# First stage in three pieces with a written TensorE order, and earlier loads in the second attention, in a two-layer decoder trunk

## Chip, cores and metric

The kernel runs on one core of a Trainium2 chip. The metric is the device time of one execution in microseconds (us), the median of several runs. Three runs of the kernel before took 2381.39, 2383.12 and 2384.1 us; the median is 2383.12 us.

## The reference

Input is x, 1024 tokens by 1024 features, in float32, with a conditioning vector c. Two layers follow each other: an mLSTM layer with a squared-ReLU MLP, then a causal latent attention (MLA) layer with another MLP. What the change touches is the first projection of layer 0, and the start of the attention for the second half of the queries.

```python
cond = jax.nn.silu(c)
ada = cond @ ada_w[l] + ada_b[l]
sh1, sc1, g1, sh2, sc2, g2 = jnp.split(ada, 6, axis=-1)
h = modulate(rmsnorm(x, norm_g[l, 0]), sh1, sc1)     # rmsnorm(x) * g * (1 + sc1) + sh1
proj = h @ w_in                                      # q, k, v, gates, output gate
...
s = q_nope . k_nope + q_rope . k_rope                # per head, causal, softmax, times v
```

So before the first product of `proj` stand: the mean square of each token's row of x, the vectors sc1 and sh1 (each a product of cond with a 1024 x 1024 block of `ada_w`, 4 MB), and x with features on the partitions (x transposed).

## The kernel before, in words

The tokens are worked in two halves of 512 (`hfs[0]`, `hfs[1]`). Activations lie with features on partitions: eight blocks of 128 features by 512 tokens. Each float32 factor is split in a high part (rounded to fp32r) and a low part (the rest), and a product is three matmuls, `mm3` (L234 to L236): activation high by weight low, activation low by weight high, high by high. `wsplit` (L190) makes the parts of a weight block of 128 x 1024: ScalarE casts it (L192), VectorE subtracts (L193). `split_mod` (L470) does the same for an activation: ScalarE scales and rounds (L476), VectorE makes the low part (L477).

The order of each engine's instructions is made by a scheduler from the order of the program, from priorities and from `tc.issue_after`, which keeps an instruction behind another of the same engine. All loads and stores of this text are issued by SyncE (SP) in one queue, in order; a DMA waits there for the landing of the one eight places ahead of it, and for the buffer that it writes. Buffers come from pools: `k4` (24 of 4 KB a partition), `hd` (8), `raw` (4, weights as loaded), `ws` (8, weight parts), `tmc`, `tmp`, `tma`, and in PSUM `ps` (2 banks), `pc` (2 banks), `pm` (2 of 2 banks).

Stage one, up to the last row of `qk_pairs` (L572):
- `load_x(0)` (L293) loads four blocks of 128 tokens by 1024 features, 512 KB each. `rms_x0` (L507) squares each on ScalarE; `along_tokens` (L490, L495) lays the token's factor along the free dimension.
- `first_norm` (L1680): 32 transposes on TensorE (`turn`, L530), four to a PSUM bank of `pc`; ScalarE copies each bank out (L1687).
- `ada_first(j)` (L1671) for j = 0 and 1, each for 512 of the 1024 features. The sum for sc1 (SC1) is made on VectorE, `ada_chunk` (L351): eight accumulating operations of 128 x 512 (L361, L363), after which four one-column matmuls with `ones` add over the partitions (`ada_turn`, L336). The sum for sh1 (SH1) is made on TensorE, `ada_chunk_pe` (L316, L324). The loads of both alternate.
- `modulate0(j)` (L1690): for each of four blocks of features a multiplication on VectorE (L1697), then `split_mod`.
- `qk_pairs` (L572): six accumulators of 128 x 512 (q0 to q3, k0, k1; four in `pm`, two in `ps`), first over the four feature blocks of j = 0, then over those of j = 1, from three pairs of weight blocks of 256 columns: 144 matmuls.

`vector_columns` (L280) transposes the rows of norm gains and biases (st1, st2) into columns. After stage one the transposed x is stored to memory (L1773), and gates, the last q and k, v and the chunks follow.

The second attention: `attention_second` (L1559) prepares the second half's k, v and queries of the eight heads in pairs (`prepare_pair`, L1415). A pair stores its parts of k (kd, L1430), of v (vd, L1436), of the queries (qd, L1452) and of the rotary queries (td, L1453). After the fourth pair, `units` takes the heads one by one; `loaded_head` (L1460) loads all of a head's k (two loads, L1465), its queries (L1467), for an even head the pair's rotary queries (L1470), and v (two loads, L1473). The first score products (L1368 to L1374) read these. Dense MLP products of the first half are put between the steps of the attention.

Of the kernel before, what the change touches and what calls it, by code (L numbers as in the profile page):

```python
# [82 lines left out]
def kernel(  # L83
# [51 lines left out]
    def tmp(dt=F32):  # L135
        return sb.tile([P, 512], dt, tag="tmp", bufs=TMP, name=f"tmp_{next(uid)}")
# [91 lines left out]
    def wcols(w, c0, n=P, k0=0, nk=KD):  # L228
        return w[k0 * P : (k0 + nk) * P, c0 : c0 + n].rearrange("(k p) n -> p k n", p=P)
# [47 lines left out]

    cols = const([P, 200], F32, "cols")

    def vector_columns():  # L280
        for i, st in ((0, st1), (1, st2)):
            pt = ps()
            nc.tensor.transpose(pt[:, :P], st[:, :P], ident)
            n = min(P, 200 - i * P)
            nc.vector.tensor_copy(cols[:, i * P : i * P + n], pt[:, :n])

    col = lambda i, n: cols[:, i : i + n]
    NG = lambda l, i: col(l * 32 + i * 8, 8)
# [24 lines left out]
    ada = const([P, 2, 48], F32, "ada")  # L313
    kvada = const([P, 16], F32, "kvada")

    def ada_chunk_pe(w, c0, bias, dst, buf):  # L316

        rows = pc()
        for q in range(4):
            r = buf()[:, :1024].rearrange("p (a b) -> p a b", b=512)  # L320
            nc.sync.dma_start(r, wcols(w, c0, 512, 2 * q, 2))
            for kk in range(2):
                k = 2 * q + kk
                nc.tensor.matmul(  # L324
                    rows[ts(k % 4, 32)], condw[:, k], r[:, kk], start=k < 4, stop=k >= 4
                )
            yield
        acc = tmp()
        nc.scalar.copy(acc, rows)
        yield from ada_turn(acc, bias, dst, True)  # L330

    def ada_turn(acc, bias, dst, alone):
        pt = pc()
        if alone:
            for j in range(4):
                ada_last[0] = nc.tensor.matmul(  # L336
                    pt[:, j : j + 1], acc[:, ts(j, P)], ones[:, 0:1], start=True, stop=True
                )
            ada_sum[0] = nc.vector.tensor_add(dst, pt[:, :4], bias)
            yield  # L340
            return
        for j in range(4):
            ada_last[0] = nc.tensor.transpose(pt[:, ts(j, P)], acc[:, ts(j, P)], ident)
# [5 lines left out]
    ada_last, ada_sum = [None], [None]  # L349

    def ada_chunk(w, c0, bias, dst, buf=raw):  # L351

        acc = tma() if buf is raw else tmc()
        for q in range(4):
            r = buf()[:, :1024].rearrange("p (a b) -> p a b", b=512)
            nc.sync.dma_start(r, wcols(w, c0, 512, 2 * q, 2))
            for kk in range(2):
                k = 2 * q + kk
                with paced():
                    if k == 0:  # L360
                        nc.vector.tensor_scalar(acc, r[:, kk], cond[:, 0:1], None, ALU.mult)  # L361
                    else:
                        nc.vector.scalar_tensor_tensor(  # L363
                            acc, r[:, kk], cond[:, k : k + 1], acc, ALU.mult, ALU.add
                        )
            yield
        if buf is raw:
            yield
            yield "wait"
        yield from ada_turn(acc, bias, dst, buf is not raw)  # L370

    def ada_part(l, part, buf=raw, js=(0, 1), how=ada_chunk):
        for j in (2 * part + js[0], 2 * part + js[-1])[: len(js)]:
            yield from how(
                ada_w[l], j * 512, col(AB + l * 48 + j * 4, 4), ada[:, l, ts(j, 4)], buf
            )

    def ada_kv(part):
# [111 lines left out]
    def along_tokens(dst, y):  # L490


        pt = pc()
        for t in range(4):
            nc.tensor.matmul(  # L495
                pt[:, ts(t, P)], y[:, t : t + 1].to_broadcast([P, P]), ident, start=True, stop=True
            )
        nc.scalar.copy(dst, pt)
        return dst
# [68 lines left out]

    def w_qk(b, kh, load=wload):
        return load([(0, 0, wcols(w_in, b * 256, 256, 4 * kh, 4))], 256)  # L570

    def qk_pairs(hf, w0, ahead):  # L572


        h = hf.h
        hf.q = [k4v(), k4v()]
        hf.k = [k4v(), k4v()]
        m0, m1 = pm(), pm()
        acc = [(m0[:, 0], m0[:, 1]), (m1[:, 0], m1[:, 1]), (ps(), ps())]

        def half(b, kh, w):
            for r in range(2):
                for k in range(4):
                    kk = 4 * kh + k
                    mm3(
                        acc[b][r], w[0][:, k, ts(r, P)], w[1][:, k, ts(r, P)], h.hi[kk], h.lo[kk],
                        kk == 0, kk == KD - 1,
                    )

        half(0, 0, w0[0])  # L590
        with tc.issue_after(ada_last[0].ins):
            for b in range(1, 3):
                half(b, 0, w0[b])
        yield from ahead
        for b in range(3):
            half(b, 1, w_qk(b, 1, wload_late))
            for r in range(2):
                qk_evac(hf, 2 * b + r, acc[b][r])
            yield

    def qk_last(hf):
        h, acc = hf.h, (ps(), ps())
# [1065 lines left out]

    A0 = mods[:, 0]

    def ada_first(j, buf):  # L1671

        a_, b_ = ada_part(0, SC1, buf, (j,)), ada_part(0, SH1, buf, (j,), ada_chunk_pe)
        yield from weave(a_, b_, 1.0)
        s = ts(j, 4)
        nc.vector.scalar_tensor_tensor(
            A0[:, s], adac(0, SC1)[:, s], 1.0, NG(0, 0)[:, s], ALU.add, ALU.mult
        )

    def first_norm():  # L1680

        y = rms_x0(x0)
        xT = FH(claim=True)
        for k in range(KD):
            pt = pc()
            turn(x0, pt, k)
            nc.scalar.copy(xT[k], pt)  # L1687
        return xT, along_tokens(Cst.rearrange("p a b -> p (a b)")[:, :H], y)

    def modulate0(h, xT, j):  # L1690
        A, sh = A0, adac(0, SH1)

        behind = [None, ada_sum[0].ins]
        for k in range(4 * j, 4 * j + 4):
            u = tmc()
            with tc.issue_after(behind[k % 4]) if behind[k % 4] else nullcontext():
                nc.vector.scalar_tensor_tensor(u, xT[k], A[:, k : k + 1], rs0, ALU.mult, ALU.mult)  # L1697
            split_mod(h.hi[k], h.lo[k], u, sh[:, k : k + 1])
            behind.append(nc.cur_bb.bb.instructions[-1])
            yield  # L1700

    def w_raw(b):
        r = raw()
        nc.sync.dma_start(
            r.rearrange("p (a b) -> p a b", b=256), wcols(w_in, b * 256, 256, 0, 4)
        )
        return r

    def w_parts(r):
        return [t.rearrange("p (a b) -> p a b", b=256) for t in wsplit(r, D)]  # L1710

    vector_columns()
    xT0, rs0 = first_norm()
    drain(ada_first(0, k4))

    w0 = [w_raw(b) for b in range(3)]
    hfs[0].h = Split()
    w0[0] = w_parts(w0[0])
    drain(modulate0(hfs[0].h, xT0, 0))
    traced = nc.cur_bb.bb.instructions  # L1720
    with tc.issue_after(next(i for i in reversed(traced) if i.engine == dve)):
        w0[1:] = [w_parts(r) for r in w0[1:]]
    drain(ada_first(1, hd))

    def with_bg(g, bg, n):
        acc = 0.0
# [41 lines left out]
        drain(wide)  # L1768

    bgs = chain(bg0, bg1)  # L1770
    drain(qk_pairs(hfs[0], w0, modulate0(hfs[0].h, xT0, 1)))
# [239 lines left out]
```

## Time and profile before

| what | value |
|---|---|
| runs, median | 2383.12 us |
| profiled execution, its own time | 2388.66 us |
| its span | 2386.9 us |
| mean granted clock of TensorE | 0.996 |
| idle before the first transposes (x), four times | 3.8 us |

The page gives the busy time of each engine: PE is TensorE's matmuls, PEld its weight loads, DVE VectorE, ACT ScalarE, POOL GpSimd, and SPq SyncE's queue of DMA issues. A row of a timeline has start and duration in us, engine, line, operation, output <- inputs, shape and count, and in brackets the idle time before it and what ended it. A row of busy time by stretch has the stretch, its length, then for each engine (PE, PEld, DVE, ACT, POOL) busy us and the number of instructions, then the granted clock, the DMA engines' busy share and GB/s. A matmul's duration covers its way through the array, so rows that follow each other overlap; the distance of their starts is the pitch.

### The profile page before, as it was taken

What the parts mean: (1) busy time and instruction counts of PE and PEld (TensorE: products, weight loads), DVE (VectorE), ACT (ScalarE), POOL (GpSimd) and SP (SyncE); (2) the same over time, 40 slices, a digit from 0 to 9 for tenths busy, and PEclk for the clock granted to TensorE, in tenths of its full rate; (3) what the DMA queues carried; (4) which work ended last, traced back from release to release, by engine and by line L of the source; (5) the groups of instructions that cost most, each with busy time, mean ns of one, the idle gap of its engine ahead of it and who ended that gap; (6) DMA issues with size and microseconds to landing.
All of it is one profiled execution on the core that took longest, in us unless ns stands there. A gap on an engine that the chain in (4) does not pass through costs nothing.

```text
span 2386.9 us, 30478 instructions
## 1 busy us (share of the span) xinstructions
PE 2356.2 (99%) x11585; PEld 1939.7 (81%) x11585; DVE 1542.5 (65%) x2430; ACT 1057.0 (44%) x1726; POOL 17.0 (1%) x91
## 2 busy tenths in 40 slices
PE   8999999999999999999999999999999999999998
PEld 5888888888878887888888788878888888888886
DVE  6666776868665768777765877656666495353345
ACT  4354435655333454443443554434444353444333
POOL 1000000000000000000000000000000000000000
PEclk9999999999999999999999999999999999999999
DMA  8543454545563845555543544764434354354431
GB/s 309 170 126 111 143 171 142 168 139 161 176 193 109 273 152 167 166 155 174 178 133 116 164 160 152 252 230 135 137 98 156 102 166 133 102 185 141 145 98 62
DMA packets 376563, 372.91 MB, mean 156 GB/s; under 512 B 24323, under 2 KB 282432, under 8 KB 376416
## 3 DMA queue, kind: packets, MB, share of 16 engines
q1 hardware_dynamic: 376128, 370.86, 49.6%
q8 instruction: 91, 1.49, 0.3%
q14 instruction: 56, 0.46, 0.1%
q0 software_dynamic: 288, 0.10, 0.0%
HBM read 312.19 MB, written 58.72 MB: 155 GB/s over the span
## 4 chain that ended last, share of the span: by engine, by line
PE 85%; DMA 6%; DVE 5%; ACT 2%; issue 2%; SPq 0%; DVEq 0%; ACTq 0%
PE ps L234 16%; PE ps L235 15%; PE ps L236 15%; PE pm L234 9%; PE pm L235 9%; PE pm L236 9%; DMA raw<-in_mlp_w_dram 4%; DVE wl L193 1%; PE pc L1488 1%; ACT wh L192 1%; DVE tma L363 1%; PE pm L1374 1%; PE pc L234 1%; PE pc L235 1%; PE pc L236 1%
## 5 line engine op out<-in xcount | busy, mean ns | idle before, releaser
L193 DVE TENSOR_TENSOR wl<-raw,wh 128x1024 fp32r<-128x1024 f32 (+3 forms) x368 | 439.2, 1197 | 446.5 <-ACT wh L192 444.0
L192 ACT CAST wh<-raw 128x1024 fp32r<-128x1024 f32 (+3 forms) x368 | 376.8, 1028 | 731.6 <-PE ps L234 374.2
L234 PE MATMUL ps<-k,wl 128*128 128x512 f32 x1496 | 597.8, 400 | 1.0 <-DVE wl L193 0.9
L236 PE MATMUL ps<-k,wh 128*128 128x512 f32 x1496 | 588.1, 393 | 0.0
L235 PE MATMUL ps<-k,wh 128*128 128x512 f32 x1496 | 587.2, 392 | 0.0
L234 PEld LDWEIGHTS ps<-k,wl 128*128 128x128 f32 x1496 | 281.0, 188 | 65.9 <-issue 2.7
L236 PEld LDWEIGHTS ps<-k,wh 128*128 128x128 f32 x1496 | 280.9, 188 | 65.9 <-issue 0.2
L235 PEld LDWEIGHTS ps<-k,wh 128*128 128x128 f32 x1496 | 281.4, 188 | 61.8 <-issue 1.4
L201 DVE TENSOR_TENSOR k<-k,pm 128x512 f32<-128x512 f32 (+1 forms) x254 | 211.1, 859 | 97.0 <-PE pm L236 96.4
L234 PE MATMUL pm<-hd,wl 128*128 128x512 f32 x512 | 201.5, 394 | 0.4 <-ACT hd L473 0.4
L236 PE MATMUL pm<-hd,wh 128*128 128x512 f32 x512 | 200.1, 391 | 0.0
L235 PE MATMUL pm<-hd,wh 128*128 128x512 f32 x512 | 199.8, 391 | 0.2 <-DVE hd L474 0.2
L234 PE MATMUL pm<-wh,hd 128*128 128x512 f32 x488 | 192.5, 394 | 1.7 <-ACT raw L1380 1.3
L235 PE MATMUL pm<-wl,hd 128*128 128x512 f32 x488 | 191.2, 392 | 0.0
L236 PE MATMUL pm<-wh,hd 128*128 128x512 f32 x488 | 190.2, 390 | 0.0
L363 DVE SCALAR_TENSOR_TENSOR tma<-raw,cond,tma 128x512 f32<-128x512 f32 x168 | 125.5, 747 | 25.5 <-DMA raw<-in_kv_ada_w_dram 13.3
L474 DVE TENSOR_TENSOR hd<-tmp,hd 128x512 fp32r<-128x512 f32 x128 | 88.3, 690 | 53.7 <-ACT hd L473 53.3
L1380 ACT ACTIVATE raw<-pm,sm 128x128 f32<-128x128 f32 (+3 forms) x64 | 47.5, 742 | 155.0 <-DVE sm L1379 121.0
L234 PEld LDWEIGHTS pm<-hd,wl 128*128 128x128 f32 x512 | 96.1, 188 | 21.9 <-ACT hd L473 0.8
L235 PEld LDWEIGHTS pm<-hd,wh 128*128 128x128 f32 x512 | 96.1, 188 | 21.5 <-DVE hd L474 0.5
L236 PEld LDWEIGHTS pm<-hd,wh 128*128 128x128 f32 x512 | 96.1, 188 | 20.7
L234 PEld LDWEIGHTS pm<-wh,hd 128*128 128x128 f32 x488 | 91.6, 188 | 23.0 <-ACT raw L1380 3.8
(350 smaller groups left out, 3451.7 us busy)
## 6 DMA issues: line engine op xcount, KB each, us to landing
raw<-in_mlp_w_dram SPq DMA_DIRECT2D x256, 512.0 KB, 4.2
raw<-in_ada_w_dram SPq DMA_DIRECT2D x80, 512.0 KB, 4.3
raw<-in_a_w_in_dram SPq DMA_DIRECT2D x44, 512.0 KB, 4.3
xs<-k SPq DMA_DIRECT2D x40, 256.0 KB, 4.5
raw<-in_a_w_out_dram SPq DMA_DIRECT2D x16, 512.0 KB, 4.8
raw<-in_kv_ada_w_dram SPq DMA_DIRECT2D x16, 512.0 KB, 3.9
kd<-k SPq DMA_DIRECT2D x32, 256.0 KB, 4.3
vd<-k SPq DMA_DIRECT2D x32, 256.0 KB, 4.7
```

Of the source, the lines that this page charges most:

```text
L192: nc.scalar.copy(hi[:, :n], r[:, :n])
L193: i = nc.vector.tensor_sub(lo[:, :n], r[:, :n], hi[:, :n].bitcast(F32))
L201: return f(*a, **k)
L234: nc.tensor.matmul(o, ll, rh, start=start, stop=False)
L235: nc.tensor.matmul(o, lh, rl, start=False, stop=False)
L236: pe_last[0] = nc.tensor.matmul(o, lh, rh, start=False, stop=stop)
L363: nc.vector.scalar_tensor_tensor(acc, r[:, kk], cond[:, k : k + 1], acc, ALU.mult, ALU.add)
L474: nc.vector.tensor_sub(lo, u, hi.bitcast(F32))
L1374: nc.tensor.matmul(o[:, :w], qh, kh, start=False, stop=True)
L1380: nc.scalar.activation(pr[:, :n], f, AF.Exp, bias=m, scale=SCALE, accum_out=l)
L1488: nc.tensor.transpose(pt[:, ts(2 * e + i, P)], u.prs[i][:, ts(b + e, P)], ident)
```

## The change

1. x of the first half is loaded in eight half blocks (first all four blocks' features 0 to 511, then 512 to 1023). The banks of the 32 transposes come from `pc` and `ps` in turn, and VectorE, no longer ScalarE, copies them out.
2. `busy(14)`: 14 bf16 matmuls of `identb` with itself, 128 x 512, whose result nothing reads, at the start of TensorE's program.
3. Stage one goes by pieces of 256, 256 and 512 features (p0, p1, p2) instead of two of 512. For each piece the loads of SC1 and SH1 alternate; the first two pieces' blocks are 256 columns wide. p0's two sums are both made on TensorE; of p1 and p2, SC1's on VectorE and SH1's on TensorE. The six accumulators are filled piece by piece: the four q tiles from weight blocks of 512 columns by two feature blocks (wA), the two k tiles from blocks of 256 columns by four (wB). TensorE's order is written out with `on_pe`. All eight blocks of SC1 and SH1 loads of p2, then the four stores of the transposed x, stand ahead of the last three weight blocks in SP's queue.
4. st2 is transposed in the middle of the stage, in a bank of `pc`; `along_tokens` takes a bank of `ps` (for the second half, too).
5. In `attention_second` the loads of head 0 are traced after the fourth pair's kd stores and ahead of its vd, qd and td stores.

The program's order on the engines after stage one is otherwise that of before.

```diff
     def load_x(half):
-        xt = []
-        for t in range(4):
-            a = k4()[:, :1024]
-            nc.sync.dma_start(a, x_of[half * 4 + t])
-            xt.append(a)
+        xt = [k4()[:, :1024] for _ in range(4)]
+        for g in range(2):
+            for t in range(4):
+                nc.sync.dma_start(xt[t][:, ts(g, 512)], x_of[half * 4 + t][:, ts(g, 512)])
         return xt
...
     def along_tokens(dst, y):
-        pt = pc()
+        pt = ps()
...
             else:
-                yield from pairs[p_]
+                yield next(pairs[p_])
+                first = loaded_head(0)
+                yield from pairs[p_]
 
         def units():
             for hh in range(NH):
-                h_ = loaded_head(hh)
+                h_ = loaded_head(hh) if hh else first
...
+    def first_turn():
+        xT = FH(claim=True)
+        for k in range(KD):
+            pt = ps() if k % 2 else pc()
+            turn(x0, pt, k)
+            nc.vector.tensor_copy(xT[k], pt)
+        return xT
...
+    class Piece:
+        def __init__(self, k0, n, buf):
+            self.k0, self.n, w = k0, n, n * P
+            m = 1024 // w
+            self.r = {}
+            for i in range(KD // m):
+                for part in (SC1, SH1):
+                    r = buf()[:, :1024].rearrange("p (a b) -> p a b", b=w)
+                    nc.sync.dma_start(r, wcols(ada_w[0], part * D + k0 * P, w, m * i, m))
...
+        def by_tensor(self, part):
+            rows = pc()[:, : self.n * P]
+            for k in range(KD):
+                nc.tensor.matmul(
+                    rows[ts(k % 4, 32)], condw[:, k], self.r[part, k], start=k < 4, stop=k >= 4
+                )
+            self.acc[part] = tmp()[:, : self.n * P]
+            nc.scalar.copy(self.acc[part], rows)
...
+    def busy(n):
+        pt = pc()
+        for _ in range(n):
+            i = nc.tensor.matmul(
+                pt, identb, identb.unsqueeze(1).to_broadcast([P, 4, P]), start=True, stop=True
+            )
+        return i.ins.engine
+
+    pe_engine = busy(14)
+    vector_columns(0, st1)
+    xT0 = first_turn()
+    p0 = Piece(0, 2, k4)
+    wA = [Weights(0, 512, 0, 2)]
+    p1 = Piece(2, 2, k4)
+    wA.append(Weights(0, 512, 2, 2))
+    wB = [Weights(512, 256, 0, 4)]
+    p2 = Piece(4, 4, hd)
...
+    rs0 = along_tokens(Cst.rearrange("p a b -> p (a b)")[:, :H], rms_x0(x0))
+    p0.by_tensor(SC1)
+    lo_of = wA[0].by_blocks()
+    next(lo_of)
+    p0.turn((SC1,))
+    p0.by_tensor(SH1)
+    p0.turn((SH1,))
+    p0.modulate(h, xT0, lo_of)
...
+    p1.by_vector(SC1)
+    wA[1].parts()
+    on_pe(some_of, wA[0], None, 0, range(4))
+    on_pe(p1.by_tensor, SH1)
+    on_pe(some_of, wA[0], None, 1, range(2))
+    on_pe(p1.turn)
+    on_pe(some_of, wA[0], None, 1, range(2, 4))
+    on_pe(vector_columns, 1, st2)
+    p1.modulate(h, xT0)
+    wB[0].parts()
+    p2.by_vector(SC1)
+    wA += [Weights(0, 512, k, 2) for k in (4, 6)]
+    wB.append(Weights(512, 256, 4, 4))
+    wA[2].parts()
+    for k in (2, 3):
+        on_pe(some_of, wA[1], None, k, range(4))
+    on_pe(p2.by_tensor, SH1)
+    on_pe(some_of, None, wB[0], 0, range(4, 6))
+    on_pe(p2.turn)
+    for k in range(1, 4):
+        on_pe(some_of, None, wB[0], k, range(4, 6))
+    p2.modulate(h, xT0)
+    wA[3].parts()
+    wB[1].parts()
+    for k in range(4, 8):
+        on_pe(some_of, wA[k // 2], None, k, range(4))
+    for k in range(4, 8):
+        on_pe(some_of, None, wB[1], k, range(4, 6))
```

`p.turn` adds over the partitions with one-column matmuls as `ada_turn` did; `p.by_vector` is the accumulation of `ada_chunk` at the piece's width; `some_of(wa, wb, k, tiles)` issues the `mm3` of one feature block k for the named accumulators; `Weights.parts` is `wsplit`, `by_blocks` the same in two halves of 512 columns.

More of the change, by code (lines that the diff above doesn't have):

```diff
@@ L278, with vector_columns @@
     cols = const([P, 200], F32, "cols")
[L280 to L285, printed above, removed]
+    def vector_columns(i, st):
+        pt = pc()
+        nc.tensor.transpose(pt[:, :P], st[:, :P], ident)
+        n = min(P, 200 - i * P)
+        nc.vector.tensor_copy(cols[:, i * P : i * P + n], pt[:, :n])
     col = lambda i, n: cols[:, i : i + n]
@@ L314, with ada_turn @@
     kvada = const([P, 16], F32, "kvada")
[L316 to L332, printed above, removed]
-        pt = pc()
[L334 to L341, printed above, removed]
+    def ada_turn(acc, bias, dst):
+        pt = pc()
         for j in range(4):
-            ada_last[0] = nc.tensor.transpose(pt[:, ts(j, P)], acc[:, ts(j, P)], ident)
+            nc.tensor.transpose(pt[:, ts(j, P)], acc[:, ts(j, P)], ident)
         s = small(4)
@@ L347, in ada_turn, with ada_chunk @@
         yield
-    ada_last, ada_sum = [None], [None]
-    def ada_chunk(w, c0, bias, dst, buf=raw):
-        acc = tma() if buf is raw else tmc()
+    def ada_chunk(w, c0, bias, dst):
+        acc = tma()
         for q in range(4):
-            r = buf()[:, :1024].rearrange("p (a b) -> p a b", b=512)
+            r = raw().rearrange("p (a b) -> p a b", b=512)
             nc.sync.dma_start(r, wcols(w, c0, 512, 2 * q, 2))
@@ L366, in ada_chunk, with ada_part @@
             yield
[L367 to L375, printed above, removed]
+        yield
+        yield "wait"
+        yield from ada_turn(acc, bias, dst)
+    def ada_part(l, part):
+        for j in (2 * part, 2 * part + 1):
+            yield from ada_chunk(
+                ada_w[l], j * 512, col(AB + l * 48 + j * 4, 4), ada[:, l, ts(j, 4)]
             )
@@ L570, in w_qk @@
         return load([(0, 0, wcols(w_in, b * 256, 256, 4 * kh, 4))], 256)
[L572 to L599, printed above, removed]
     def qk_last(hf):
@@ L1686, in first_norm @@
             turn(x0, pt, k)
[L1687 to L1720, printed above, removed]
@@ L1721, with last_on, in_order, by_vector @@
-    with tc.issue_after(next(i for i in reversed(traced) if i.engine == dve)):
-        w0[1:] = [w_parts(r) for r in w0[1:]]
-    drain(ada_first(1, hd))
+            nc.vector.tensor_copy(xT[k], pt)
+        return xT
+    def last_on(engine):
+        return next(i for i in reversed(nc.cur_bb.bb.instructions) if i.engine == engine)
+    def in_order(engine, f, *a):
+        with tc.issue_after(last_on(engine)):
+            return f(*a)
+    class Piece:
[7 more added lines that the diff above has]
+                    nc.sync.dma_start(r, wcols(ada_w[0], part * D + k0 * P, w, m * i, m))
+                    for j in range(m):
+                        self.r[part, m * i + j] = r[:, j]
+            self.acc = {}
+        def by_vector(self, part, ks=range(KD)):
+            for k in ks:
+                r = self.r[part, k]
+                if k == 0:
+                    acc = self.acc[part] = tmc()[:, : self.n * P]
+                    nc.vector.tensor_scalar(acc, r, cond[:, 0:1], None, ALU.mult)
+                else:
+                    acc = self.acc[part]
+                    nc.vector.scalar_tensor_tensor(
+                        acc, r, cond[:, k : k + 1], acc, ALU.mult, ALU.add
+                    )
[7 more added lines that the diff above has]
+            nc.scalar.copy(self.acc[part], rows)
+        def turn(self, parts=(SC1, SH1)):
+            s = slice(self.k0, self.k0 + self.n)
+            for part in parts:
+                pt = pc()
+                for j in range(self.n):
+                    nc.tensor.matmul(
+                        pt[:, j : j + 1], self.acc[part][:, ts(j, P)], ones[:, 0:1],
+                        start=True, stop=True,
+                    )
+                self.sum = nc.vector.tensor_add(
+                    adac(0, part)[:, s], pt[:, : self.n], col(AB + part * 8, 8)[:, s]
+                ).ins
+                if part == SC1:
+                    nc.vector.scalar_tensor_tensor(
+                        A0[:, s], adac(0, SC1)[:, s], 1.0, NG(0, 0)[:, s], ALU.add, ALU.mult
+                    )
+        def modulate(self, h, xT, then=None):
+            A, sh = A0, adac(0, SH1)
+            behind = [None, self.sum]
+            for i in range(self.n):
+                k = self.k0 + i
+                u = tmc()
+                with tc.issue_after(behind[i]) if behind[i] else nullcontext():
+                    nc.vector.scalar_tensor_tensor(
+                        u, xT[k], A[:, k : k + 1], rs0, ALU.mult, ALU.mult
+                    )
+                split_mod(h.hi[k], h.lo[k], u, sh[:, k : k + 1])
+                if then:
+                    in_order(dve, drain, then)
+                behind.append(nc.cur_bb.bb.instructions[-1])
@@ new lines, with __init__, parts, by_blocks @@
+    class Weights:
+        def __init__(self, c0, n, k0, m):
+            self.n, self.m, self.k0 = n, m, k0
+            self.r = raw()
+            nc.sync.dma_start(
+                self.r[:, : n * m].rearrange("p (a b) -> p a b", b=n), wcols(w_in, c0, n, k0, m)
+            )
+        def parts(self):
+            self.w = [
+                t[:, : self.n * self.m].rearrange("p (a b) -> p a b", b=self.n)
+                for t in wsplit(self.r, self.n * self.m)
+            ]
+        def by_blocks(self):
+            t = [
+                sb.tile([P, 1024], F32R, tag="ws", bufs=WS, name=f"w_{next(uid)}")
+                for _ in range(2)
+            ]
+            self.w = [a[:, : self.n * self.m].rearrange("p (a b) -> p a b", b=self.n) for a in t]
+            for k in range(self.m):
+                s = ts(k, self.n)
+                nc.scalar.copy(t[0][:, s], self.r[:, s])
+            for k in range(self.m):
+                s = ts(k, self.n)
+                yield nc.vector.tensor_sub(t[1][:, s], self.r[:, s], t[0][:, s].bitcast(F32))
@@ L1725, in with_bg @@
+    on_pe(p2.by_tensor, SH1)
[10 more added lines that the diff above has]
+        on_pe(some_of, None, wB[1], k, range(4, 6))
+    for m in range(6):
+        qk_evac(hf, m, acc[m])
     def with_bg(g, bg, n):
@@ L1770 @@
     bgs = chain(bg0, bg1)
-    drain(qk_pairs(hfs[0], w0, modulate0(hfs[0].h, xT0, 1)))
     for b in range(4):
```

26 lines of the change are left out of this document (16 added, 10 removed).

## The prediction

> **What bounds the kernel now.** I read the page first, then TensorE's waits, then busy time by stage, then the timelines of the first 70 us and of the start of the second attention.
>
> ```profile
> span 2386.9 us, 30478 instructions
> PE 2356.2 (99%) x11585; PEld 1939.7 (81%) x11585; DVE 1542.5 (65%) x2430; ACT 1057.0 (44%) x1726; POOL 17.0 (1%) x91
> ```
>
> ```profile
> PE pm L234 <- ACT k L476: 2.4, 1, 2.4
> PE pm L1370 <- DMA k<-td: 2.4, 1, 2.4
> ...
> PE pc L785 <- ACT tmc L769: 0.7, 1, 0.7
> ```
>
> ```profile
> 0.00:10.00 10.00, 3.03 (x10) 1.55 (x10) 4.05 (x22) 5.36 (x9) 6.19 (x21) 1.00 0.79 279
> 10.00:20.00 10.00, 8.91 (x45) 5.97 (x44) 5.79 (x13) 6.07 (x13) 0.00 (x0) 1.00 1.05 385
> 20.00:30.00 10.00, 7.32 (x29) 4.14 (x31) 7.88 (x15) 6.31 (x8) 0.00 (x0) 0.70 1.07 371
> 40.00:50.00 10.00, 10.00 (x38) 8.08 (x38) 8.86 (x12) 5.76 (x7) 0.00 (x0) 0.83 0.80 249
> 120.00:140.00 20.00, 18.50 (x149) 16.79 (x149) 15.23 (x26) 12.12 (x33) 0.00 (x0) 1.00 0.66 180
> 1580.00:1585.00 5.00, 5.00 (x21) 4.26 (x22) 0.98 (x2) 0.89 (x2) 0.00 (x0) 0.66 1.03 417
> ```
>
> TensorE is busy 2356.2 of 2386.9 us, so only 30.7 us of idle time and the matmuls run at a low granted clock (the column after the busy times) can be won. The first two waits belong to the places that the change touches: 2.4 us before the first product of stage one (L476) and 2.4 us in the second attention (td). The clock is low in 20 to 30 us, 40 to 50 us and 1580 to 1585 us: the same places. Everywhere else the order of instructions on TensorE, VectorE and ScalarE stays as it was, apart from a few neighbours near 150 us and 1595 us, so what is won or lost at these places passes to the end.
>
> ```profile
> 9.52 0.69 PE L530 MATMUL pc<-ident,k 128*128 128x128 f32 x2 [0.58 <-DMA k<-in_x_dram]
> 11.23 5.66 PE L530 MATMUL pc<-ident,k 128*128 128x128 f32 x24 [1.02 <-ACT k L1687]
> 16.77 1.33 PE L495 MATMUL pc<-ident,sm 128*128 128x128 f32 x8
> 18.03 1.91 PE L324 MATMUL pc<-k,tma 128*32 128x512 f32 x12
> 22.21 1.03 PE L336 MATMUL pc<-ones,tmp 128*128 128x1 f32 x8
> 25.61 0.79 PE L234 MATMUL pm<-k,wl 128*128 128x512 f32 x1 [2.37 <-ACT k L476]
> ...
> 38.28 1.02 PE L336 MATMUL pc<-ones,tmc 128*128 128x1 f32 x8 [0.59 <-DVE tmc L363]
> ...
> 41.49 0.63 PE L236 MATMUL pm<-k,wh 128*128 128x512 f32 x1
> 41.92 0.63 PE L234 MATMUL pm<-k,wl 128*128 128x512 f32 x1
> ...
> 45.17 0.39 PE L234 MATMUL pm<-k,wl 128*128 128x512 f32 x1
> 45.40 0.39 PE L235 MATMUL pm<-k,wh 128*128 128x512 f32 x1
> ...
> 69.05 0.40 PE L236 MATMUL ps<-k,wh 128*128 128x512 f32 x1
> ```
>
> Stage one runs to 69.28 us (the last row's start plus one pitch). Its 144 products start every 0.43 us at the low clock (41.49 to 41.92) and every 0.23 us at the full one (45.17 to 45.40).
>
> **The change, front.** Bytes stay the same. x still lands whole at 9.52 us.
>
> ```profile
> 13.51 1.54 DVE L363 SCALAR_TENSOR_TENSOR tmc<-k,cond,tmc 128x512 f32<-128x512 f32 x2 [0.89 <-DMA k<-in_ada_w_dram]
> ...
> 18.99 1.54 DVE L363 SCALAR_TENSOR_TENSOR tmc<-k,cond,tmc 128x512 f32<-128x512 f32 x2 [1.15 <-DMA k<-in_ada_w_dram]
> ```
>
> Four 512 KB blocks land between these two waits: 1.37 us each. Counting from 9.52 us in the new order, the first piece (4 blocks) is there at 15.0, the first weights at 16.4, the second piece at 21.8, its weights at 24.6, the third piece (8) at 35.5. Then the xT stores (4), now ahead of the last three weight blocks, put these at 42.4, 43.7 and 45.1.
>
> The added filler is 14 matmuls of 512 columns, behind one transpose that the program puts ahead of them and that waits for the first half block of x (about 4.4 us, half a block before the 5.10 us of now). At 0.23 to 0.43 us each they end between 7.6 and 10.5 us. The clock column says 1.00 there, but the transposes contradict it:
>
> ```profile
> L530 PE MATMUL pc<-ident,k 128*128 128x128 f32 x32 | 8.4, 433 | 4.9 <-DMA k<-in_x_dram 3.8 <-ACT k L1687 1.0
> L530 PE MATMUL ps<-ident,k 128*128 128x128 f32 x32 | 5.0, 279 | 0.0
> ```
>
> Those of the first stage take 433 ns, the same shape later 279, and 24 of them need 5.66 us. So the array starts at half speed; I take 10.5 us for the filler. That costs nothing much, as x lands at 9.52 us. It pays by warming the array: 31 transposes at some 0.13 us instead of 0.24.
>
> The eight copies out of PSUM move from ScalarE (582 ns) to VectorE:
>
> ```profile
> L1687 ACT COPY k<-pc 128x512 f32<-128x512 f32 x8 | 4.7, 582 | 2.0 <-PE pc L530 2.0
> ```
>
> ```profile
> L697 DVE COPY tmc<-pc 8x512 f32<-8x512 f32 x2 | 1.4, 682 | 0.0
> L477 DVE SCALAR_TENSOR_TENSOR k<-tmc,ada,k 128x512 fp32r<-128x512 f32 x16 | 12.0, 748 | 5.0 <-ACT k L476 4.6
> L1382 DVE TENSOR_SCALAR raw<-raw,sm 128x256 f32<-128x256 f32 x8 | 2.8, 353 | 0.3
> ```
>
> 0.68 us each, with a pitch of about 0.61. First copy at 10.5 + 1.0 (eight transposes); the SC1 product reuses the bank of the seventh copy: 11.5 + 7 x 0.61 + 0.5 (three small operations between) = 16.3 us. From there the chain of the first piece: SC1 product 0.9 (half of the 512-wide one, whose rows span 18.03 to 21.3 with a wait), row statistics 1.2, its turn 0.5 (half of L336's 1.03), SH1 product 0.9, copy 0.4, turn 0.5, addition 0.2, scaled block on ScalarE 0.72, hand-overs: the first product starts at about **21.9 us instead of 25.61**.
>
> **The change, from 21.9 us to the stage's end.** Work on TensorE: 144 x 0.228 = 32.8, SH1 of the pieces 0.9 + 1.7, turns 0.9 + 1.8, st2's transpose 0.1: 38.2 us. The waits come from VectorE, which stands in its own order:
> - the second piece's sum. Between 21.1 and its end VectorE does one modulation 0.67, eight 256-wide operations (the form is not in the trace; between 0.35 and 0.75, I take 0.46 from the ratio of its 256- and 512-wide neighbours) 3.7, two low parts 1.35, one 512-wide difference 0.6, two 1024-wide ones 2.3: 29.6 us. TensorE has 18 products, SH1 and waits until 27.3: 2.3 us idle.
> - low parts of blocks 0 and 2, high part of block 2: 0.4 + 0.7 + 0.4.
> - after the third piece's SC1 turn VectorE has three small operations (0.5), six 512-wide ones (4.2 with the waits for ScalarE) and a 1024-wide difference (1.2) up to the low half of the third weight block, 6.0 us; TensorE has the SH1 turn and 18 products, 5.0: 1.1 idle, at about 47.5. That block landed at 42.4, so the 5.5 us of xT stores moved ahead of it stay hidden; without that cover each us is the stage's.
>
> 38.2 + 4.9 = 43.1, the stage ends at **65.0 us** at full clock. VectorE, not the transfers, is the stage's new bound.
>
> **The clock.** Now: TensorE had 2.37 us of idle and one-column products before 25.61, and the clock was 0.70; 0.59 us of idle and 1.9 us of one-column products before 40, and it was 0.83; 2.36 us of idle before 1579.91, and it was 0.66. One fall of some 3.4 us costs (1 - 0.66) x 5 = 1.7 us of work. After the change there are three thin stretches: the copies until 16.3, the first piece's turns until 21.9, the wait at 27.3 to 29.6. I count 1.9 us, one fall and a bit, with ends 0 and 5 (three falls). Stage one: 66.9 us, 2.4 us won, between -1 and +5.
>
> The Trainium skill ("TensorE: Matmul & The Clock Gate", section "Why this matters for your kernels") asks only that no TensorE gap exceeds about 3 us. The row at 1580 speaks against it: a gap of 2.36 us was enough. By the Trainium skill no gap left after the change would lower the clock, and stage one would end near 65.0 us.
>
> **The change, second attention.**
>
> ```profile
> 1577.16 0.39 PE L1369 MATMUL pm<-k,k 128*128 128x512 f32 x1
> 1579.91 0.50 PE L1370 MATMUL pm<-hd,k 128*128 128x512 f32 x1 [2.36 <-DMA k<-td]
> ```
>
> ```profile
> 1552.26 2.72 SPq L1430 DMA_DIRECT2D kd<-k  x4
> 1562.78 2.33 SPq L1436 DMA_DIRECT2D vd<-k  x4
> 1565.21 3.54 SPq L1452 DMA_DIRECT2D qd<-k  x2
> ...
> 1570.72 0.36 SPq L1470 DMA_DIRECT2D k<-td  x1
> ```
>
> ```profile
> 1550.00:1555.00 5.00, 5.00 (x23) 4.05 (x23) 3.97 (x7) 2.82 (x5) 0.20 (x1) 1.00 0.60 212
> 1555.00:1560.00 5.00, 5.00 (x31) 4.42 (x30) 2.79 (x5) 1.13 (x2) 0.00 (x0) 1.00 0.33 121
> 1560.00:1565.00 5.00, 5.00 (x28) 4.31 (x28) 3.94 (x5) 2.63 (x4) 0.00 (x0) 1.00 0.26 72
> ```
>
> The td load is issued at 1570.72, behind ten stores, and lands at 1579.9. Now the six loads of head 0 (3 MB) go among the kd stores, from about 1553 us, into a stretch where the DMA engines are 33 and 26% busy; at 385 GB/s they need 8 us, landing by 1563 or so, 13 us before use. They need buffers that were given free long before. The wait of 2.36 us goes, and with it the fall of the clock (1.7): **4.0 us**, ends 0 and 4.1. Next in line is the first unit's softmax, which has 24 dense products of 0.23 us over it, as now. Other edits (st2's columns and the row statistics in another PSUM pool) cost nothing beside dense products; without that cover, a few tenths.
>
> **Sum.** 2.4 + 4.0 = 6.4 us. The profiled execution took 2388.66 (span 2386.9 and 1.8 around it) and would take 2382.3; the runs' median is 2383.12, so I predict 2383.1 - 6.4 = **2376.7 us**.
>
> **Rivals.**
> - No fall of the clock in stage one, since its gaps are spread over several stretches: 69.28 - 65.0 = 4.3, with 4.0 is 8.3, 2374.8 us. For it: 1.5 us of gaps in 120 to 140 us (0.7 of it at L785) leave the clock at 1.00. Against: the 1580 row. It is also what the Trainium skill's limit on gaps, cited above, would give.
> - The clock stays low through most of stage one, since each piece has its thin stretch: three falls, stage one ends at 70, one lost; with 4.0 won elsewhere 2380.2 us.
> - The new loads don't do what they say: the wait moves from td to another transfer of the same head, and only stage one pays: 2380.7 us.
> - Slower: the 3 MB of loads delay the kd stores behind them in SP's queue. The buffer of the last pair's first q is now that of a kd store, so ScalarE's copy of q waits for the store to land. The copy follows those of v, whose stores start at 1562.78, so it stands near 1563.5; the stores are issued until 1555 and would land, with 2 us of added issue and 1.5 MB (4 us) ahead, by 1561 to 1564. From 1566 on each us is TensorE's, as two PSUM banks fill up. Landing at 1573 it loses 7 with a fall of the clock, and the 2.4 of stage one against it: 2387.7 us.
>
> **Chances.** Forecast 0.54, no fall 0.15, low clock 0.17, loads 0.08, slower 0.06. About 0.2% (4.8 us) is what a measurement tells from no change. Faster by more: the first two cases, 0.69. Within: low clock and loads, 0.25. Slower: 0.06. The range takes the forecast with its unknowns and the next three: 2372.5 to 2382.
>
> **What would show it.** Right: the first product at 21 to 23 us; a wait of 1 to 2.5 us for the second piece's sum; the stage's last product at 64 to 69; no td wait and a clock of 1.00 around 1580. Wrong: half clock in 30 to 50 us, VectorE's 256-wide operations near 0.75 us, weights later than 47 us, or ScalarE waiting for a kd store near 1563.

## The result and the profile after

The changed kernel takes 2395.57 us (median of 6 runs, 2392.7 to 2396.97); the kernel before, in runs beside it, 2384.18 us (2381.39 to 2386.13). The ratio is 1.0045, 95% interval 1.0035 to 1.0055: 10.7 us slower, between 8.3 and 13.1. The profiled execution took 2392.7 us, its span is 2390.9.

The head of the page, after:

```profile
span 2390.9 us, 30582 instructions
PE 2365.7 (99%) x11631; PEld 1938.9 (81%) x11631; DVE 1545.2 (65%) x2442; ACT 1052.6 (44%) x1721; POOL 16.9 (1%) x91
```

Idle time of TensorE fell from 30.7 to 25.2 us. But its busy time rose by 9.5 us, and the 46 matmuls more do not explain that: all of them lie in stage one, up to whose end TensorE is busy 58.0 us before and 58.3 after. Behind it both kernels run 11,334 matmuls, and there the other 9 us arose. So TensorE's own work has become slower somewhere, and a list of waits will not show where. First the places that the change touches. TensorE's waits, after:

```profile
PE pm L234 <- ACT raw L1322: 2.5, 4, 1.1
PE pc L1664 <- DVE k L1622: 1.3, 1, 1.3
...
PE pm L234 <- ACT k L447: 1.0, 1, 1.0
...
PE pm L234 <- DVE wl L193: 0.8, 1, 0.8
...
PE pc L1675 <- DVE tmc L1657: 0.5, 1, 0.5
```

The first product's wait of 2.4 us is down to 1.0, and the wait for td isn't in the list at all. Busy time by stretch, after:

```profile
10.00:20.00 10.00, 7.91 (x57) 5.64 (x56) 6.18 (x15) 5.05 (x13) 0.00 (x0) 0.85 1.09 357
20.00:30.00 10.00, 8.50 (x58) 5.77 (x58) 8.23 (x18) 4.89 (x8) 0.00 (x0) 0.81 1.07 368
...
40.00:50.00 10.00, 10.00 (x60) 6.90 (x58) 6.03 (x12) 4.33 (x6) 0.00 (x0) 1.00 0.81 284
...
1580.00:1585.00 5.00, 5.00 (x23) 4.06 (x23) 2.20 (x6) 0.99 (x2) 0.00 (x0) 1.00 0.87 269
```

Up to the last products the recorded clock is low only in 10 to 30 us (two windows of 3.41 us, from 16.92 and 23.75), and it is full at 1580. TensorE's timeline of stage one, after:

```profile
16.78 1.85 PE L1664 MATMUL pc<-k,tma 128*32 128x256 f32 x16 [1.34 <-DVE k L1622]
...
24.00 1.22 PE L234 MATMUL pm<-k,w 128*128 128x512 f32 x2 [1.01 <-ACT k L447]
...
31.60 0.58 PE L1675 MATMUL pc<-ones,tmc 128*128 128x1 f32 x4 [0.53 <-DVE tmc L1657]
...
50.95 0.50 PE L234 MATMUL pm<-k,wl 128*128 128x512 f32 x1 [0.79 <-DVE wl L193]
...
67.93 0.39 PE L234 MATMUL ps<-wh,k 128*128 128x272 f32 x1
```

The last row is the first product after the stage: the stage ends at 67.93 us, 1.35 earlier than before (69.28). So both places were won in this execution, and the loss must lie in code that the change leaves as it was. To find it, the same product is looked up in both timelines. Before:

```profile
1600.74 0.40 PE L1368 MATMUL pm<-k,k 128*128 128x512 f32 x1
...
2138.05 0.39 PE L234 MATMUL pm<-wh,hd 128*128 128x512 f32 x1
...
2143.51 0.39 PE L234 MATMUL ps<-k,wl 128*128 128x512 f32 x1
...
2367.34 0.39 PE L235 MATMUL pc<-wl,hd 128*128 128x512 f32 x1
```

After:

```profile
1595.63 0.40 PE L1310 MATMUL pm<-k,k 128*128 128x512 f32 x1
...
2138.62 0.40 PE L234 MATMUL pm<-wh,hd 128*128 128x512 f32 x1
...
2144.22 0.40 PE L234 MATMUL ps<-k,wl 128*128 128x512 f32 x1
...
2371.37 0.39 PE L235 MATMUL pc<-wl,hd 128*128 128x512 f32 x1
```

The first pair: 1600.74 before, 1595.63 after, so 5.1 us ahead. The last pair: 4.0 us behind. 9.1 us are lost between these rows, at full clock. The middle pairs show most of it: between their two rows lie 24 products of the second MLP, of weights and hd tiles, without a gap. They take 5.46 us before (227.5 ns each) and 5.60 us after (233.3 ns). Between the first and the last pair stand 1,320 such products; at 5.8 ns each they make 7.7 of the 9.1 us. A page of means hides this, since a row's duration rose by 5 ns in 390.

### The profile page after: what moved, and what is told of

The parts are those of the page before. It is cut to its first block, busy times and chain, and to the rows that moved or that the text cites. A ratio compares the mean times of both kernels' runs of the same rounds, so it can differ in the third digit from the quotient of the medians.

```text
span 2390.9 us, 30582 instructions
## 1 busy us (share of the span) xinstructions
PE 2365.7 (99%) x11631; PEld 1938.9 (81%) x11631; DVE 1545.2 (65%) x2442; ACT 1052.6 (44%) x1721; POOL 16.9 (1%) x91
## 4 chain that ended last, share of the span: by engine, by line
PE 91%; DVE 4%; DMA 2%; ACT 1%; issue 1%; SPq 0%; DVEq 0%; ACTq 0%
PE ps L234 16%; PE ps L235 16%; PE ps L236 16%; PE pm L234 10%; PE pm L235 10%; PE pm L236 10%; PE pc L1430 1%; PE pm L1316 1%; DVE wl L193 1%; PE pc L234 1%; PE pc L235 1%; PE pc L236 1%; PE pm L1310 1%; PE pm L1313 1%; PE pm L1311 1%
## 5 line engine op out<-in xcount | busy, mean ns | idle before, releaser
L234 PE MATMUL pm<-wh,hd 128*128 128x512 f32 x488 | 195.0, 400 | 2.8 <-ACT raw L1322 2.5
L236 PE MATMUL pm<-wh,hd 128*128 128x512 f32 x488 | 192.9, 395 | 0.0
```

Source lines behind the costliest of these rows:

```text
L234: nc.tensor.matmul(o, ll, rh, start=start, stop=False)
L236: pe_last[0] = nc.tensor.matmul(o, lh, rh, start=False, stop=stop)
```

## Experiments

### Where the buffers stand

The change adds no work there, but it asks for buffers in another order. A pool gives a ring its place when the first buffer of it is asked for. In the program before, SBUF has the small columns, tmc, weight parts (at byte 162336 of the partition) and hd (195104). After the change, the third piece asks for hd first, and the order is hd (149856), small columns, weights (182816), tmc. In PSUM `pc` and `pm` change places. Theory A: the places in SBUF set the pitch. Theory B: the PSUM banks do. Theory C: something of the new order of work does, such as the traffic.

First run: the instructions of the changed kernel in the same order, the rings asked for as before.

```diff
+    def place(ring, n):
+        for _ in range(n):
+            ring()
+    def ws():
+        return sb.tile([P, 1024], F32R, tag="ws", bufs=WS, name=f"ws_{next(uid)}")
+    place(lambda: small(4), 6)
+    place(tmc, TMC)
+    place(ws, WS)
     pe_engine = busy(14)
```

> The changed kernel with the same instructions in the same order; only the rings of SBUF buffers are asked for in the order of before, so that the hd, weight and tmc tiles stand at the addresses that they had before (PSUM as after the change). Theory A (the places in SBUF of the weights and the hd tiles against each other set the pitch of the late products): the pitch of the products of hd and weight tiles falls from 233 back to 227 ns, some 1,500 of them, and the time is 2378 to 2386 us, at or below before. Theory B (the PSUM banks do it) and theory C (something of the new order of work, such as the traffic, does it): 2395 us as after the change, pitch 233 ns.

Measured: 2386.68 us; ratio to before 1.0007 (0.9998 to 1.0016). The pitch of those products is 227.7 ns again. Nine us of the loss are gone without one instruction moved.

Second: only the PSUM rings as before (`place(pm, 2)` in place of the three lines).

> The changed kernel with only the PSUM rings placed as before (the double banks at 2 and 4, not at 4 and 6), SBUF as after the change. Theory A (places in SBUF): no change, 2395 us, pitch of the late products 233 ns. Theory B (PSUM banks): 2378 to 2386 us, pitch 227 ns. Theory C (new order of work): 2395 us.

Measured: 2393.71 us, ratio 1.0037 (1.0024 to 1.005). The pitch stays at 233.4 ns, so theory B falls.

Third: the kernel before, with nothing of the change but its places.

```diff
+    ...                                  # place() and ws() as in the first run
+    place(hd, HD)
+    place(lambda: small(4), 6)
+    place(ws, WS)
     vector_columns()
     xT0, rs0 = first_norm()
```

> The kernel before, none of the change in it, with its SBUF rings asked for in the order of the changed kernel, so that hd, weight and tmc tiles stand where the change put them. Theory A (places in SBUF): 8 to 12 us slower than before, 2392 to 2396 us, pitch of the products of hd and weight tiles in the second MLP 233 instead of 227 ns. Theories B and C: 2384 us and 227 ns.

Measured: 2392.68 us, ratio 1.003 (1.0019 to 1.0041): 7.2 us slower, between 4.5 and 9.8; pitch 233.3 ns. Theory C falls: the old work at the new places has the slow pitch. Groups by line, first run:

```profile
L235 PE MATMUL pm<-hd,wh 128*128 128x512 f32 x512 | 199.7, 390 | 0.2 <-DVE hd L445 0.2
...
L235 PE MATMUL pm<-wl,hd 128*128 128x512 f32 x488 | 191.1, 392 | 0.0
```

Third run:

```profile
L235 PE MATMUL pm<-hd,wh 128*128 128x512 f32 x512 | 200.4, 392 | 0.2 <-DVE hd L474 0.2
...
L235 PE MATMUL pm<-wl,hd 128*128 128x512 f32 x488 | 193.2, 396 | 0.0
```

The second row of each counts the second MLP (weights move through the array, hd stands in it): 392 and 396 ns. The first row is the first MLP, where hd moves and the weights stand: 390 and 392.

What in the places? Weights and hd lay 32768 bytes apart before and 32960 after, which is 0 and 192 modulo 256. Five more runs of the kernel before with other rings between hd and the weights; this is the one with dec:

```diff
+    ...                                  # place() and ws() as in the first run
+    place(hd, HD)
+    place(lambda: const_rot("dec", [P, 4, 4]), 2)
+    place(ws, WS)
+    place(lambda: small(4), 6)
```

Between the two stand nothing (distance 0), the two gc tiles (256 modulo 512), dec (128), inv and sg (64), or small columns and dec (320 modulo 512).

> The kernel before with its SBUF rings asked for in a third order: hd, then the weight tiles right behind it, then the small columns and tmc. hd and weights stand in the order of the changed kernel, at absolute addresses of its kind, but their distance is 32768 bytes as before, not 32960. Theory A1 (the distance of the two rings modulo 512 bytes sets the pitch): 227.8 ns for the products of hd and weight tiles in the second MLP and 2384 to 2386 us. Theory A2 (which ring lies lower, or the absolute place, sets it): 233.3 ns and 2392 us.

> The kernel before with its SBUF rings in the order hd, the two gc tiles, weights, small columns, tmc: the distance of weights and hd is 33536 bytes, 256 modulo 512. Theory A1 as stated (only a distance of 0 modulo 512 is quick): 231 to 236 ns for the products of hd and weight tiles in the second MLP, 2389 to 2394 us. Weaker form (a multiple of 128 or 256 is enough, and 192 is slow because it is none): 227 to 229 ns and 2384 to 2387 us.

> The kernel before, rings in the order hd, the two dec tiles, weights, small columns, tmc: distance of weights and hd 128 modulo 512. Read from it is only the pitch of the products of hd and weight tiles in the second MLP. If a distance that is a multiple of 128 bytes is quick (0 and 256 are, 192 is not): 227 to 229 ns. If only multiples of 256 are: 231 to 236 ns.

> The same with the two single columns inv and sg between hd and weights: distance 64 modulo 512. Odd multiples of 64 are slow (192 is): 231 to 236 ns. If 192 is slow by itself and 64 is not: 227 to 229 ns.

> The same with small columns and dec between hd and weights: distance 320 modulo 512, which is an odd multiple of 64 and 192 taken the other way round. Odd multiples of 64 are slow: 231 to 236 ns. Otherwise 227 to 229 ns.

Measured, as the mean distance of starts in ns over some 1,400 neighbouring products of each kind (in brackets the distance of the two rings, moving minus standing operand, modulo 256 bytes):

| run | weights move, hd stands | hd moves, weights stand | time, us |
|---|---|---|---|
| before | 227.7 (0) | 228.4 (0) | 2384.2 |
| distance 0, hd below | 228.3 (0) | 227.9 (0) | 2386.75 |
| distance 256 | 228.2 (0) | 227.9 (0) | 2388.38 |
| distance 64 | 229.2 (64) | 233.3 (192) | 2394.1 |
| distance 320 | 229.2 (64) | 233.3 (192) | 2394.52 |
| distance 128 | 232.8 (128) | 232.9 (128) | 2400.22 |
| before at new places | 233.3 (192) | 229.5 (64) | 2392.68 |
| changed kernel | 233.3 (192) | 229.2 (64) | 2395.57 |

The times stand beside 2384.2 to 2385.8 us of before. In the last five rows the values agree to 0.3 ns wherever the bracket is the same, whichever operand moves, and in different kernels. Of the distances tried, only multiples of 256 are quick. Theory A1 is right in kind, but its modulus was wrong: 256, not 512. A2 (the lower ring, or the absolute place) falls with the second row. Distances 64, 128 and 320 have one run each and so no interval, but their sums fit. For 128, 1,536 products of each kind times 5.1 + 4.5 ns are 14.7 us, where 16.0 were measured. For 64 and 320 the sum is 9.8 us, where 9.9 and 10.3 were measured. For 192 it fits less well: 10.3 us, where the third run has 7.2 (4.5 to 9.8). Groups by line for 128:

```profile
L235 PE MATMUL pm<-hd,wh 128*128 128x512 f32 x512 | 202.0, 395 | 0.2 <-DVE hd L474 0.2
...
L235 PE MATMUL pm<-wl,hd 128*128 128x512 f32 x488 | 193.4, 396 | 0.0
```

And for 64:

```profile
L235 PE MATMUL pm<-hd,wh 128*128 128x512 f32 x512 | 202.1, 395 | 0.2 <-DVE hd L474 0.2
...
L235 PE MATMUL pm<-wl,hd 128*128 128x512 f32 x488 | 191.9, 393 | 0.0
```

At 128 both rows are slow, at 64 the first one alone. Left open: the two quick distances are still 2.6 us (0.5 to 4.8) and 2.1 us (0 to 4.3) above before. Their products of k and weight tiles took about 0.4 ns longer (231.6 ns in both, 231.1 before; some 4,600 of them, about 2 us). But for k, whose buffers stand 4160 bytes apart, the table's rule does not hold. In the kernel before, as it is built, the distances of these products take all four values modulo 256, and the mean pitch at 0, 64, 128 and 192 is 231.2, 231.2, 231.4 and 230.8 ns. What sets it is open.

### The early loads alone

The kernel before with edit 5 of the change, nothing else:

```diff
+                yield next(pairs[p_])
+                first = loaded_head(0)
                 yield from pairs[p_]
...
-                h_ = loaded_head(hh)
+                h_ = loaded_head(hh) if hh else first
```

> The kernel before with one part of the change, the loads of head 0 of the second attention ahead of the last stores. By the prediction's step the wait for td (2.4 us) and the fall of the clock at 1580 us (1.7) go: 4.0 us faster, 2380 us. If the wait only moves to another transfer of the head: 2383 to 2384 us. If the loads hold up the stores of k: 2386 us or more.

Measured: 2383.84 us, ratio 0.9995 (0.9986 to 1.0004): 1.2 us faster, from 3.3 faster to 1.0 slower. In its trace there is no wait for td and no fall of the clock near 1580 us. So the wait goes as forecast, and its price was wrong: the eight traces with the late loads show waits for td of 2.4, 0.6, 0.7, 1.6, 1.1, 1.1, 0.4 and 2.0 us, mean 1.2. The clock fell at 1580 us in two of them, those with 2.4 and 2.0.

### The new stage one alone

The first run without edit 5 (its lines as in before).

> The changed kernel at the SBUF places of before, without the early loads of the second attention: the new first stage alone. By the prediction's step stage one gains 2.4 us: 2382.4 us. Theory D (the gain was read from one execution of before with four windows of half clock; the new stage, with its thin stretches, has on average more such windows than the old one, and at full clock the two stages end within half a us of each other): no gain, 2385 to 2389 us, and a lower mean granted clock than before over the runs.

Measured: 2387.92 us, ratio 1.0013 (1.0004 to 1.0021): 3.1 us slower than before, between 1.0 and 5.0. Theory D holds for the time, but its reason is not shown. The mean granted clock over its 11 runs is 0.9965, over the 27 of before beside it 0.9970: 8.5 against 7.1 us of span lost. These means count full clock up to the first entry of the clock's record, which stands at 14.7 to 17.2 us in eight traces of the old stage and at 6.8 to 10.2 us in four of the new one, so they don't compare like with like. From there to the end of the stage the eight traces have 22 low windows of 3.41 us (2.75 each), the four 10 (2.5 each): not more.

In its trace the stage ends at 67.86 us, as in the three other traces of the new stage (67.86 to 68.32; eight traces of the old one 69.09 to 70.13). By these traces the stage itself is 1.4 us shorter, and what the edit costs over the runs is lost behind it. The td row, with the wait back again:

```profile
1578.96 0.50 PE L1312 MATMUL pm<-hd,k 128*128 128x512 f32 x1 [2.02 <-DMA k<-td]
```

That wait does not explain the 3.1 us, as the kernel before has it, too; where they are lost stays open. This trace waits 1.8 and 1.0 us for VectorE between 135 and 720 us, the early-loads trace 1.4 us for ScalarE; such waits come and go in both kernels.

### Filler in the gaps

The first run with 16 more filler products in TensorE's gaps. To place them, the run also fixes TensorE's order there and puts the row statistics behind the first piece's SC1 product:

```diff
-    xT0 = first_turn()
+    ...                                  # first_turn, in three parts
+    m0, m1 = pm(), pm()
+    turned_of((4, 5))
+    in_pe(filled, 3)
+    in_pe(turned_of, (6, 7))
+    in_pe(filled, 5)
...
+    in_pe(filled, 2)                     # behind p0's SC1 product, ahead of the row statistics
...
+    in_pe(filled, 2)                     # ahead of SH1's turn
+    in_pe(p0.turn, (SH1,))
+    in_pe(filled, 4)                     # ahead of the first product
```

> The changed kernel at the SBUF places of before, with 16 further filler products (identity, 512 columns, into a PSUM bank that is free until the first product) in the gaps of TensorE between 14 and 24 us: 3 and 5 between the turns of x, 2 behind the SC1 product, 2 and 4 ahead of the turn of SH1 and the first product. Theory D (half-clock windows in the thin stretches of stage one cost the gain, 1.7 us each): the falls at 17 and 24 us go, mean granted clock 0.998 or more over the runs, 2380 to 2384 us. If the clock is not the cause: 2386 us or, with the filler in the way, up to 2388 us.

Measured: 2381.41 us, ratio 0.9994 (0.9985 to 1.0003); mean granted clock 0.9979 where the first run had 0.9966. Each beside its own runs of before, the first run is 1.7 us slower and this one 1.4 us faster. So some 3 us came from work that computes nothing and the order around it. The one trace does not show this gain: the first product starts at 22.66 instead of 23.93, but the stage ends at 68.78 instead of 67.86. What then ends TensorE's longest wait is the sum that the prediction had named:

```profile
31.31 0.84 PE L1675 MATMUL pc<-ones,tmc 128*128 128x1 f32 x4 [2.64 <-DVE tmc L1657]
```

2.64 us (2.3 forecast), with half clock from 31.47 to 38.3 behind it. In the changed kernel TensorE came later, after two windows of half clock, and waited only 0.53 us here.

Then that sum on TensorE:

```diff
-    p1.by_vector(SC1)
+    on_pe(p1.by_tensor, SC1)
...
-    wB[0].parts()
+    in_order(nc.scalar.engine, wB[0].parts)
```

> The kernel of the filler run, and the sum of SC1 of the second piece on TensorE (16 products of 256 columns) instead of VectorE, with the cast and low part of the first 256-wide weight block behind the second piece. In the filler run TensorE waited 2.64 us for that sum on VectorE and the clock fell for two windows right behind it. Theory D (VectorE's sum and the half-clock windows are what is left): this wait goes under 0.6 us, no fall at 31 us, 3 us less than the filler run: a median of 2377 to 2380 us, below before in every run. Rival: the transfers set the second piece anyway (its last block lands near 24 us) and another wait takes its place: 2381 us as in the filler run.

Measured: 2382.31 us against 2385.76 for before beside it, ratio 0.9987 (0.9978 to 0.9996): 3.1 us faster than before, between 1.0 and 5.2, the only version whose interval lies below 1. Busy time by stretch:

```profile
10.00:20.00 10.00, 7.37 (x63) 5.00 (x65) 5.59 (x15) 5.63 (x14) 0.00 (x0) 1.00 1.09 355
20.00:30.00 10.00, 9.82 (x80) 5.75 (x76) 5.12 (x10) 3.89 (x7) 0.00 (x0) 1.00 1.07 370
30.00:40.00 10.00, 9.58 (x49) 6.45 (x52) 9.47 (x17) 2.32 (x3) 0.48 (x5) 1.00 1.05 392
```

The clock is full in these stretches, the mean over the runs 0.9989. The wait for the second piece is gone, a low weight part takes 1.4 us in its place later in the stage, and the stage ends at 66.62. Of the 3 us below the filler run the ratios to before (0.9987 against 0.9994) show 1.7, which the scatter of the runs doesn't tell from none. In the traces it is 2.2 us ahead of the filler run at 62 us and level at 1610. Between 70 and 950 us its TensorE waits 1.5 us for VectorE's background sums and 1.8 us for a low weight part (0.5 and 1.3 in the filler run). So in this trace what was won early was given back behind the stage, in part to VectorE.

## Why the prediction was wrong

**The sum, by experiments.** New places +7.2 us (third run), new stage one +3.1, early loads -1.2: together 9.1, measured 10.7 (8.3 to 13.1). The prediction had nothing for the first, -2.4 for the second, -4.0 for the third. The second is what its edit costs over the runs; the stage itself is shorter in the traces.

**The step that failed first** stands in the opening: "Everywhere else the order of instructions on TensorE, VectorE and ScalarE stays as it was, [...] so what is won or lost at these places passes to the end." The order did stay. The time of the instructions did not, because the new code asks for its buffers in another order. No rival had this; "slower" was given to a stall that the trace after does not show (ScalarE never waited for a kd store).

**The second, the clock.** "I count 1.9 us, one fall and a bit" was set against an execution with three low windows in stage one. They cost it (1 - 0.70) x 10, (1 - 0.96) x 10 and (1 - 0.83) x 10 = 5.1 us between 20 and 50 us, or 4.3 without the 1.6 us of half clock in which TensorE still waited for its first product. By this estimate the old stage ends at 64.2 to 65.0 us at full clock. My 65.0 for the new one at full clock was no gain at all; the whole "2.4" was fewer falls. They did not come: four traces of the new stage have 2.5 low windows on the mean, where 1.9 us at 1.7 each stand for 1.1. The stage still ends 1.4 us earlier in the traces (68.0 against 69.4 on the mean), but the runs of its edit alone are 3.1 us slower, and that cause stays open. Of the rivals, the one with low clock through the stage was the nearest; it had 0.17.

**The third, the price of the td wait.** "4.0 us, ends 0 and 4.1": the profiled execution of before had the longest wait of eight and a fall. It was an outlier as a whole: 2388.66 us, where the 72 runs beside the experiments lie between 2379.6 and 2388.86. Taking the medians as the base and one slow execution as the source of the savings counted its bad luck with td as gain.

**Right**: the SC1 product at 16.3 (16.78 measured); 256-wide operations on VectorE of 0.46 us (0.48); the wait for the second piece's sum as the next limit (2.3, and 2.64 as soon as the clock is full); the low part of the third weight block (1.1, 0.79); no td wait and full clock at 1580 in the trace after. **Off**: the first product, 24.00 instead of 21.9, as the clock fell at 16.92 in the middle of its chain (22.66 in the filler run, at full clock there); that wait for the second piece's sum in the changed kernel itself, 0.53 where 1 to 2.5 was named; the last three weight blocks, landed at 44.9, 46.6 and 48.0 instead of 42.4 to 45.1, the last behind the 47 named as a sign of being wrong, though TensorE waited for none of them. By the limit on gaps of the Trainium skill ("TensorE: Matmul & The Clock Gate", section "Why this matters for your kernels"; about 3 us) no fall was due. The trace after has two, right behind a gap of 1.34 us and within one of 1.01 us, so the measurement decides against it here, too.

## What to carry to other kernels

Before a change is priced by its own instructions, compare where the built program puts every ring of buffers, before and after: a new first request can move rings that the change does not touch, and on this kernel 64 bytes more in the distance of two rings cost ten us (9.9 and 10.3, one run each). For two rings whose tiles meet in long runs of matmuls try a distance that is a multiple of 256 bytes: for hd and weights it was quick, for k it made no difference. Measure the pitch, not the mean duration. Price a wait or a fall of the clock only from several executions: one profile is one draw.

## What the runs showed of the hardware

- The pitch of the 512-column fp32r products of hd and weight tiles, dense and at full clock, depends on the distance of the moving and the standing operand in the partition, modulo 256 bytes: 227.7 to 228.4 ns at 0, 229.2 to 229.5 at 64, 232.8 to 232.9 at 128, 233.3 at 192 (table above). Products of k and weight tiles do not follow it (230.8 to 231.4 ns at the four distances in the kernel before). What in the chip does this isn't settled. The Trainium skill ("SBUF — State Buffer", section "Who interferes with whom") gives TensorE one read port for the moving operand and one for the weight load, and calls them independent. The third run speaks against full independence: the same instructions, 5.6 ns apart.
- With useless matmuls in TensorE's gaps of 0.5 to 1.3 us, and its order fixed around them, the mean granted clock of the whole execution rose from 0.9966 to 0.9979, and to 0.9989 with the 2.64 us wait removed.
- Executions of one program differ by up to 9 us (before: 2379.6 to 2388.4 in one set of 23 runs).
